# Small matmuls of a token mixer on halves and quarters of TensorE, two DMA queues at the start, and one norm's total in another PSUM bank

## The chip, the cores and the metric

One core of one Trainium2 chip runs the whole program once per launch. The metric is the time of one execution in microseconds, measured on the device; lower is better. The engines are TensorE (PE, with its weight loads shown apart as PEld), VectorE (DVE), ScalarE (ACT), GpSimd (POOL) and SyncE (SP), which issues most DMAs.

## The reference, cut to what matters

Two transformer-like layers run on 16 learned meta tokens and 256 real tokens of width 1024, all in float32.

```python
# layer 1: the mixer, then the expert layer
proj = rmsnorm(h, norm1_g) @ w_in     # 1024 -> q,k,v (8 heads x 64), q,k (4 x 64), v, gate (4 x 128), 16 low-rank gate inputs
log_1m  = where(mask, log_sigmoid(-z), 0)              # stick-breaking attention: z = q k^T / 8, strictly causal
between = cumsum(log_1m, reverse) - log_1m
sb_o    = where(mask, exp(log_sigmoid(z) + between), 0) @ v
lg      = log_sigmoid(glr @ w_gate_up + b) / 16        # glr: the 16 low-rank gate inputs
gla_o   = gated_linear_attention(q / 8, k, v, lg)      # decays are exp of differences of cumsum(lg)
h += concat(rmsnorm(sb_o), rmsnorm(gla_o) * silu(gate)) @ w_out
h += peer_ffn(rmsnorm(h, norm2_g))                     # scores of 2 x 8 x 128 sub-keys, top 16 of 256 pairs, 16384 experts
# layer 2, on the meta tokens of its own and rmsnorm(h, norm_f_g)
q, k, v, q_idx, k_idx, w_idx, conv..., gates... = split(rmsnorm(h, norm_mix_g) @ w_in_2)
sel   = top_k(sum_heads(relu(q_idx k_idx^T) * w_idx), 68)   # which keys a query may see
mixed = sigmoid(ga) * (attention(q, k, v, sel) @ w_attn_out) + sigmoid(gb) * (short_conv(...) @ w_conv_out)
h += mixed @ w_out;  h += (silu(f @ w_gate) * (f @ w_up)) @ w_down;  return rmsnorm(h)
```

## The kernel before

Activations lie transposed: 128 features on the partitions, tokens in the columns. A large product is made from halves: ScalarE casts a weight unit of 128x1024 from `raw_t` to fp32r (`hi_t`, L209), VectorE makes the rest (`lo_t`, L211), and TensorE adds three products per 128 rows, hi·hi, hi·lo and lo·hi (`mm3`, L226 to L228). A projection of 128 output columns is so 24 matmuls (`proj`, L230). Small products (attention scores, weighted values, transposes) run on plain float32, where each matmul of the program stands as two instructions in the trace.

The program is one stream without loops on the chip. A scheduler orders the instructions of each engine by its own estimates of durations, from the order in which the code is written and from the buffers that the pools give; engines then run their rows strictly in that order. Only the expert stage's VectorE part and the end of the expert stage are pinned by hand.

The start (L352 to L372) loads the gains `vec`, then the tokens `hx` in four pieces, with the first two weight units among them, all on SP's queue; `Feed.gains` (L1330) makes the halves `u` of the tokens and `Feed.then` (L1336) the squares, whose total (L1346) gives the norm's factor `rn`. A projection doesn't wait for `rn`: its result is multiplied by it afterwards (`put`, L404).

`mix_heads` (L374) first makes the gate `sil` (four projections, units 20 to 23), then the 16 low-rank inputs `glr` from a unit padded to 128 columns (L492), and from these the decays (L498). Then its loop over c (L603) interleaves value projections, one stick-breaking head at a time (`sb_head`, L431: three score matmuls L438 to L440 with 64 rows of contraction, the weights, three value matmuls L461 to L463) and the levels of the gated linear attention. `gla_head` (L591) sums four products per head, the first with only 16 rows of contraction (L595). Heads 6 and 7 come in the tail, beside the output projection.

The expert stage starts with eight projections and the sub-key scores (`scores`, L672), whose PSUM tiles come from the pool `pep` of two banks (L833). In layer 2, `norm_mix_scale` (L1088) takes two banks `st_t` at once, one for the total of the second norm and one (`ps2`) for that of the first norm, which `first()` fills only at the eighth k projection (L1164). The selection (`select`, L962) takes its banks `lg_t` from the pool that is opened after it (L1151).

Of the kernel before, what the change touches and what calls it, by code (L numbers as in the profile page):

```python
# [8 lines left out]
F32 = mybir.dt.float32  # L9
# [4 lines left out]
OP = mybir.AluOpType  # L14
# [85 lines left out]
def arrange(i):  # L100
# [12 lines left out]
    o["w1"] = _units(np.concatenate([w, np.zeros((D, 112), np.float32)], 1))  # L113
    o["wgu"] = np.ascontiguousarray(a["w_gate_up"][0])
# [22 lines left out]
class Net:  # L137
# [236 lines left out]
    def mix_heads(self, pool, tmp, feed, hx, h1, follow):  # L374
# [14 lines left out]
        glr = hp.tile([NM, L], F32, name="glr")  # L389
# [32 lines left out]
        def turned():  # L422
            for vf, c, blocks in waiting:
# [3 lines left out]
                for i, (dst, a, n) in enumerate(blocks):  # L427
                    nc.scalar.copy(dst[:, c * 128:(c + 1) * 128], tp[:n, i * 128:(i + 1) * 128])
            waiting.clear()

        def sb_head(h):  # L431

            c, pb = h // 2, 64 * (h % 2)
            P = slice(pb, pb + 64)
            k, q = sbk[P, c, :], sbq[P, c, :]
            z = bank("z")
            zz = z[:, 0:416]
            nc.tensor.matmul(z[:, 0:256], k[:, 0:128], q, start=True, stop=True)  # L438
            nc.tensor.matmul(z[:, 256:400], k[:, 128:256], q[:, 112:256], start=False, stop=True, skip_group_check=True)
            nc.tensor.matmul(z[:, 400:416], k[:, 144:272], q[:, 240:256], start=False, stop=True, skip_group_check=True)  # L440
# [17 lines left out]
            nc.scalar.activation(a, a, AF.Exp)  # L458
            o = bank("o")
            cs = slice(c * 128, (c + 1) * 128)  # L460
            nc.tensor.matmul(o[:, 0:256], sv[0][:, cs], a[:, 0:256], start=True, stop=True)  # L461
            nc.tensor.matmul(o[:, 112:256], sv[1][:, cs], a[:, 256:400], start=False, stop=True, skip_group_check=True)
            nc.tensor.matmul(o[:, 240:256], sv[2][:, cs], a[:, 400:416], start=False, stop=True, skip_group_check=True)  # L463
            nc.vector.tensor_copy(osb[P, c, :], o[P, 0:256])

# [23 lines left out]
        wgu = hp.tile([16, 256], F32, name="wgu")  # L489
        nc.sync.dma_start(wgu, t["wgu"])  # L490

        put(glr, self.proj(t["w1"][24], x, L)[:16, :], 0)  # L492
# [37 lines left out]
        am = pool.tile([NM, 2, 2, T], F32, name="am")  # L530
# [19 lines left out]
        def gla_pairs():  # L550
# [36 lines left out]
            for j, ps in enumerate(out):  # L587
                nc.vector.tensor_copy(am[:, j], ps[:NM])
# [14 lines left out]
        for c in range(4):  # L603
            value(8, c, [(sv[0], 0, 128), (sv[1], 128, 128), (sv[2], 144, 128)])
            next(gla, None)
            if c:
                sb_head(2 * c - 2)
# [3 lines left out]
            if c:  # L611
                sb_head(2 * c - 1)
# [12 lines left out]
        with tc.tile_pool(name="mxa", bufs=1, space=PSUM) as pacc:  # L625
# [13 lines left out]
            sb_head(6)  # L639
            mix_out(0)  # L640
            gla_head(2)
            sb_head(7)
# [179 lines left out]
    def experts(self, h, follow):  # L822
# [4 lines left out]
        with ExitStack() as es:  # L827
# [5 lines left out]
            psp = xs.enter_context(tc.tile_pool(name="pep", bufs=2, space=PSUM))  # L833
# [254 lines left out]
    def norm_mix_scale(self, psp):  # L1088
# [3 lines left out]
        ps, ps2 = (psp.tile([128, 512], F32, name="st_t", tag="st") for _ in range(2))  # L1092
# [8 lines left out]
        def first():  # L1101
            sq = self.sq
# [284 lines left out]
```

## Time and profile before

| what | us |
|---|---|
| median of 3 runs (lowest, highest) | 1440.45 (1439.87, 1441.21) |
| the profiled execution's own time | 1440.71 |
| its span in the trace | 1438.9 |
| TensorE busy, of the span | 1419.5 |
| VectorE busy | 1126.8 |
| ScalarE busy | 769.4 |

The span begins with the first instruction of any engine. Matmuls overlap one another, so a busy time near the span doesn't say that TensorE is at its peak; what a matmul costs in a stream is read from the distance between the starts of neighbouring rows. The stages are the mixer to about 165 us, the experts to about 940 us, and layer 2 after that.

### The profile page before, as it was taken

The numbers are of one execution on the slowest core, as the hardware profiler recorded it, in microseconds if no ns is written. First come the engines' busy times: TensorE is split into PE (matmuls) and PEld (weight loads), VectorE is DVE, ScalarE is ACT, GpSimd is POOL, SyncE is SP. The second block draws the span as 40 slices with busy tenths as digits, with TensorE's granted clock in tenths as the row PEclk, the third lists the DMA queues.
The fourth block names the chain that finished last, engine by engine and source line by source line (L and its number), as shares of the span: only waits on it lengthen the run. The fifth ranks groups of instructions, "written<-read, shape, count | busy, mean of one in ns | idle before, by whom it ended". The sixth has DMA issues, their size and how long they took to land. (4 is left out here: it accounts for less than half of the span.)

```text
span 1438.9 us, 25131 instructions
## 1 busy us (share of the span) xinstructions
PE 1419.5 (99%) x9846; PEld 1302.0 (90%) x9846; DVE 1126.8 (78%) x1920; ACT 769.4 (53%) x1241; POOL 0.2 (0%) x4
## 2 busy tenths in 40 slices
PE   7999999999999999999999999999999999999998
PEld 7998999999999999888888888898999888989997
DVE  6975889989979998687777777798767768776665
ACT  6656654445456665545445444554445556755554
POOL 0000000000000000000000000000000000000000
PEclk9999999999999999999999999999999999999999
DMA  7322556666655555787777777744533555565552
GB/s 280 118 103 95 166 173 227 229 227 225 218 190 187 193 184 190 244 257 251 244 242 241 241 241 240 234 144 147 171 137 132 178 189 193 174 220 190 181 187 72
DMA packets 86631, 279.05 MB, mean 194 GB/s; under 512 B 9760, under 2 KB 10480, under 8 KB 86384
## 3 DMA queue, kind: packets, MB, share of 16 engines
q1 hardware_dynamic: 77296, 260.67, 54.7%
q10 hardware_dynamic: 9216, 16.78, 3.1%
q8 instruction: 77, 1.26, 0.4%
q14 instruction: 42, 0.34, 0.1%
HBM read 259.52 MB, written 17.83 MB: 193 GB/s over the span
## 5 line engine op out<-in xcount | busy, mean ns | idle before, releaser
L211 DVE TENSOR_TENSOR lo_t<-raw_t,hi_t 128x1024 fp32r<-128x1024 f32 x456 | 554.4, 1221 | 137.0 <-ACT hi_t L209 134.6
L209 ACT CAST hi_t<-raw_t 128x1024 fp32r<-128x1024 f32 x456 | 476.2, 1049 | 302.9 <-PE mm_t L227 219.1
L226 PE MATMUL mm_t<-yh,hi_t 128*128 128x256 f32 x1024 | 292.9, 286 | 0.0
L228 PE MATMUL mm_t<-yh,lo_t 128*128 128x256 f32 x1024 | 290.3, 284 | 0.2 <-DVE lo_t L211 0.2
L227 PE MATMUL mm_t<-yl,hi_t 128*128 128x256 f32 x1024 | 289.8, 283 | 0.0
L312 PE MATMUL acc<-hi_t,vl_t 128*128 128x512 f32 x512 | 199.6, 390 | 0.0
L311 PE MATMUL acc<-lo_t,vh_t 128*128 128x512 f32 x512 | 199.5, 390 | 0.0
L310 PE MATMUL acc<-hi_t,vh_t 128*128 128x512 f32 x512 | 199.5, 390 | 0.0
L228 PEld LDWEIGHTS mm_t<-yh,lo_t 128*128 128x128 f32 x1024 | 196.3, 192 | 1.1 <-DVE lo_t L211 0.9
L227 PEld LDWEIGHTS mm_t<-yl,hi_t 128*128 128x128 f32 x1024 | 196.5, 192 | 0.1
L226 PEld LDWEIGHTS mm_t<-yh,hi_t 128*128 128x128 f32 x1024 | 196.4, 192 | 0.2
L246 PE MATMUL mm_t<-oo,hi_t 128*128 128x512 f32 x384 | 135.5, 395 | 0.0
L218 ACT CAST vh_t<-va_t 128x512 fp32r<-128x512 f32 x64 | 39.7, 621 | 152.2 <-DVE va_t L932 149.6
L311 PEld LDWEIGHTS acc<-lo_t,vh_t 128*128 128x128 f32 x512 | 96.1, 188 | 20.5 <-DVE lo_t L211 0.5
L312 PEld LDWEIGHTS acc<-hi_t,vl_t 128*128 128x128 f32 x512 | 96.1, 188 | 20.4 <-DVE vl_t L219 0.6
L310 PEld LDWEIGHTS acc<-hi_t,vh_t 128*128 128x128 f32 x512 | 96.1, 188 | 19.9
L226 PE MATMUL mm_t<-u,hi_t 128*128 128x272 f32 (+1 forms) x352 | 103.3, 295 | 7.9 <-ACT hi_t L209 7.5
L228 PE MATMUL mm_t<-u,lo_t 128*128 128x272 f32 (+1 forms) x352 | 102.4, 292 | 0.5 <-DVE lo_t L211 0.5
L227 PE MATMUL mm_t<-u,hi_t 128*128 128x272 f32 (+1 forms) x352 | 101.8, 290 | 0.0
L246 PE MATMUL mm_t<-oo,lo_t 128*128 128x256 f32 x384 | 100.4, 282 | 0.3 <-DVE lo_t L211 0.3
L246 PE MATMUL mm_t<-ax,hi_t 128*128 128x512 f32 x256 | 92.9, 399 | 0.0
L246 PEld LDWEIGHTS mm_t<-oo,hi_t 128*128 128x128 f32 x384 | 70.6, 188 | 12.7
(399 smaller groups left out, 2524.3 us busy)
## 6 DMA issues: line engine op xcount, KB each, us to landing
raw_t<-in_eu SPq DMA_DIRECT2D x128, 512.0 KB, 3.9
raw_t<-in_ev SPq DMA_DIRECT2D x128, 512.0 KB, 4.3
raw_t<-in_w2c SPq DMA_DIRECT2D x40, 512.0 KB, 3.4
act<-ge_t ACTq DMA_DIRECT2D x64, 256.0 KB, 3.3
va_t<-act SPq DMA_DIRECT2D x64, 256.0 KB, 3.2
raw_t<-in_w SPq DMA_DIRECT2D x25, 512.0 KB, 3.9
raw_t<-in_w2qkv SPq DMA_DIRECT2D x24, 512.0 KB, 4.1
raw_t<-in_wg SPq DMA_DIRECT2D x22, 512.0 KB, 3.5
```

The costliest lines, as they stand in the source:

```text
L209: nc.scalar.copy(hi, raw)
L211: nc.vector.tensor_tensor(lo, raw, hi[:].bitcast(F32), op=OP.subtract)
L218: self.nc.scalar.copy(hi, x)
L226: nc.tensor.matmul(ps, hi[:, ks], xhi[:, k, s], start=k == 0, stop=False)
L227: nc.tensor.matmul(ps, hi[:, ks], xlo[:, k, s], start=False, stop=False)
L228: nc.tensor.matmul(ps, lo[:, ks], xhi[:, k, s], start=False, stop=k == KC - 1)
L246: nc.tensor.matmul(out, w, y, start=k == 0 and out is pair, stop=k == KC - 1 and out is pair, skip_group_check=True)
L310: mm(acc[q], ah, hi, start=first, stop=False, skip_group_check=True)
L311: mm(acc[q], ah, lo, start=False, stop=False, skip_group_check=True)
L312: mm(acc[q], al, hi, start=False, stop=last, skip_group_check=True)
```

## The change

Seven edits are made together. (1) `vec` and the first weight unit (20) go on ScalarE's DMA queue, the unit in two pieces of 128x512 which are split apart from each other; the table load follows the DMA issues. (2) TensorE multiplies a tile of zeros 18 times before its first data. (3) `glr` comes from eight float32 matmuls with 32 output columns, each on one quarter of the array's columns, with unsplit weights `wlr`; the four partial sums lie on four groups of partitions and are added by the next matmul, whose weights are repeated. (4) `glr`, `gvm`, `am` and `wgu` are padded with zeros to 128 rows. (5) The scores of two stick-breaking heads are issued in turns, on the upper and the lower 64 rows, into two banks; their values are issued in turns on the left and right 64 columns of the array, into one bank that one copy empties. (6) The expert pool `pep` has four banks. (7) The first norm's total is put in a bank of the matmul pool, taken when it is needed.

```diff
@@ arrange
-    o["w1"] = _units(np.concatenate([w, np.zeros((D, 112), np.float32)], 1))
-    o["wgu"] = np.ascontiguousarray(a["w_gate_up"][0])
+    o["w1"] = _units(w[:, :3072])
+    o["wlr"] = _cols(np.concatenate([w[:, 3072:], np.zeros((D, 16), np.float32)], 1))
+    o["wgu"] = np.tile(np.concatenate([a["w_gate_up"][0], np.zeros((16, 256), np.float32)], 0), (4, 1))
@@ consts
-        nc.sync.dma_start(vec, self.t["vec"])
+        nc.scalar.dma_start(vec, self.t["vec"])
@@ mixer
-        self.act_table(LNEXP)
...
+            whi, wlo = self.turns[0]
+            self.turns = self.turns[1:] + self.turns[:1]
+            first = [self.raw.tile([128, 1024], F32, name="raw_t", tag="raw")]
+            first += [whi.tile([128, 1024], F32R, name="hi_t", tag="hi"), wlo.tile([128, 1024], F32R, name="lo_t", tag="lo")]
+            self.early.append(tuple(first[1:]))
+            w = t["w1"][20].rearrange("p k j -> p (k j)")
+            parts = [[x[:, 512 * i:512 * i + 512] for x in first] for i in range(2)]
             for k in range(0, KC, 2):
                 nc.sync.dma_start(hx[:, k:k + 2, :], t["hx"][:, k:k + 2, :])
-                if not k:
-                    self.early.append(self.unit(t["w1"][20]))
-                feed.gains((k, k + 1))
-                if not k:
-                    self.early.append(self.unit(t["w1"][21]))
+                if k < 4:
+                    nc.scalar.dma_start(parts[k // 2][0], w[:, 256 * k:256 * k + 512])
+            self.act_table(LNEXP)
+            with tc.tile_pool(name="idle", bufs=1) as ip:
+                idle = ip.tile([128, 256], F32R, name="idle")
+                nc.vector.memset(idle[:].bitcast(F32), 0.0)
+                ps = self.bank()
+                for _ in range(18):
+                    nc.tensor.matmul(ps[:, :256], idle[:, :128], idle, start=True, stop=True)
+            feed.gains((0, 1))
+            for i, (raw, hi, lo) in enumerate(parts):
+                self.split(hi, lo, raw)
+                feed.gains((2 * i + 2, 2 * i + 3))
+            feed.gains((6, 7))
+            self.early.append(self.unit(t["w1"][21]))
@@ mix_heads
-        gvm = pool.tile([NM, 512], F32, name="gvm")
+        gvm = pool.tile([128, 512], F32, name="gvm")
+        nc.gpsimd.memset(gvm, 0.0)
...
-        def sb_head(h):
...
+        def sb_scores(c):
+            zs = [bank("z") for _ in range(2)]
+            for a, n, b, m, o in ((0, 128, 0, 256, 0), (128, 256, 112, 256, 256), (144, 272, 240, 256, 400)):
+                for i, z in enumerate(zs):
+                    P = slice(64 * i, 64 * i + 64)
+                    nc.tensor.matmul(z[:, o:o + m - b], sbk[P, c, a:n], sbq[P, c, b:m], start=o == 0, stop=True, skip_group_check=True)
+            return zs
...
+        def sb_values(c, heads):
+            o = bank("o")
+            for v, b, a, n in ((sv[0], 0, 0, 256), (sv[1], 112, 256, 144), (sv[2], 240, 400, 16)):
+                for i, w in enumerate(heads):
+                    nc.tensor.matmul(o[64 * i:64 * i + 64, b:b + n], v[:, c * 128 + 64 * i:c * 128 + 64 * i + 64], w[:, a:a + n],
+                                     start=b == 0, stop=True, skip_group_check=True)
+            nc.vector.tensor_copy(osb[:, c, :], o[:, 0:256])
...
-        put(glr, self.proj(t["w1"][24], x, L)[:16, :], 0)
+        nc.vector.tensor_tensor(wlr, wlr, n1, op=OP.mult)
+        ps = self.bank()
+        for k in range(KC):
+            i = 32 * (k % 4)
+            nc.tensor.matmul(ps[i:i + 32, :L], wlr[:, k, :], hx[:, k, :], start=k < 4, stop=k > 3, skip_group_check=True)
+        put(glr, ps[:, :L], 0)
...
-        am = pool.tile([NM, 2, 2, T], F32, name="am")
+        am = pool.tile([128, 2, 2, T], F32, name="am")
+        nc.gpsimd.memset(am, 0.0)
@@ experts
-            psp = xs.enter_context(tc.tile_pool(name="pep", bufs=2, space=PSUM))
+            psp = xs.enter_context(tc.tile_pool(name="pep", bufs=4, space=PSUM))
@@ norm_mix_scale
-        ps, ps2 = (psp.tile([128, 512], F32, name="st_t", tag="st") for _ in range(2))
+        ps = psp.tile([128, 512], F32, name="st_t", tag="st")
...
-            sq = self.sq
+            sq, ps2 = self.sq, self.bank()
```

The scheduler moves rows with it. On TensorE, in the mixer's loop, heads 0 and 1 of the stick-breaking attention stood like this before (`z_t` are score banks, `o_t` value banks, `sbq` and `sbk` queries and keys, `a` the weights, `sv0` to `sv2` the values):

```order
L438 MATMUL z_t_671<-sbq_146,sbk_147 128x256
L439 MATMUL z_t_671<-sbq_146,sbk_147 128x144
L440 MATMUL z_t_671<-sbq_146,sbk_147 128x16
L226 MATMUL mm_t_700<-u_92,hi_t_703 128x256
...
L438 MATMUL z_t_757<-sbq_146,sbk_147 128x256
L439 MATMUL z_t_757<-sbq_146,sbk_147 128x144
L440 MATMUL z_t_757<-sbq_146,sbk_147 128x16
...
L461 MATMUL o_t_695<-a_692,sv0_152 128x256
L462 MATMUL o_t_695<-a_692,sv1_153 128x144
L463 MATMUL o_t_695<-a_692,sv2_154 128x16
```

and in the same place of the changed kernel:

```order
L456 MATMUL z_t_682<-sbq_174,sbk_175 128x256
L456 MATMUL z_t_683<-sbq_174,sbk_175 128x256
L456 MATMUL z_t_682<-sbq_174,sbk_175 128x144
L456 MATMUL z_t_683<-sbq_174,sbk_175 128x144
L456 MATMUL z_t_682<-sbq_174,sbk_175 128x16
L456 MATMUL z_t_683<-sbq_174,sbk_175 128x16
...
L487 MATMUL o_t_787<-a_707,sv0_180 64x256
...
L487 MATMUL o_t_787<-a_784,sv0_180 64x256
L487 MATMUL o_t_787<-a_707,sv1_181 64x144
L487 MATMUL o_t_787<-a_784,sv1_181 64x144
L487 MATMUL o_t_787<-a_707,sv2_182 64x16
L487 MATMUL o_t_787<-a_784,sv2_182 64x16
```

The score rows of the two heads now alternate in one group, while of the value rows head 0's first stands alone, 20 rows ahead of the other five.

On TensorE at the end of the expert projections, the sub-key scores (`sc_t`) stood in four groups with matmuls of the first expert block (`yh`, `yl`) between them:

```order
L684 MATMUL sc_t<-sk,pq 128x128 x8
L226 MATMUL mm_t<-yh,hi_t 128x256
L227 MATMUL mm_t<-yl,hi_t 128x256
L228 MATMUL mm_t<-yh,lo_t 128x256
L226 MATMUL mm_t<-yh,hi_t 128x256
L684 MATMUL sc_t<-sk,pq 128x128 x8
```

and in the changed kernel:

```order
L229 MATMUL mm_t<-u,lo_t 128x256
L729 MATMUL sc_t<-sk,pq 128x128 x32
L227 MATMUL mm_t<-yh,hi_t 128x256
L228 MATMUL mm_t<-yl,hi_t 128x256
L229 MATMUL mm_t<-yh,lo_t 128x256
```

All 32 now stand in one group.

On VectorE in layer 2, among the last k projections (`k` is the product with the norm's factor, `lo_t` the rest of the next weight unit), the rows were:

```order
L1159 TENSOR_TENSOR k<-mm_t,r_10904 128x272
L211 TENSOR_TENSOR lo_t<-raw_t,hi_t 128x1024
L1159 TENSOR_TENSOR k<-mm_t,r_10904 128x272
L211 TENSOR_TENSOR lo_t<-raw_t,hi_t 128x1024
L1159 TENSOR_TENSOR k<-mm_t,r_10904 128x272
```

and in the changed kernel (`sc` are selection scores, `top` and `left` its rounds of eight maxima):

```order
L1204 TENSOR_TENSOR k<-mm_t,r_10906 128x272
L1036 MAX top_11280<-left_11279 128x8
L1055 MEMSET lgs_12014 128x2x112
L1037 MATCH_REPLACE left_11279<-top_11280,left_11279 128x148
L212 TENSOR_TENSOR lo_t<-raw_t,hi_t 128x1024
L1036 MAX top_11280<-left_11279 128x8
L1055 MEMSET lgs_12015 128x2x112
L1037 MATCH_REPLACE left_11279<-top_11280,left_11279 128x148
L1204 TENSOR_TENSOR k<-mm_t,r_10906 128x272
```

The selection's first half, which stood behind the eighth k projection, now runs among the k projections.

## Rows read from the trace of the kernel before

**Rows 1.** The page's part 1 (busy, share, instructions) and the clock row of part 2.

```profile
PE 1419.5 (99%) x9846; PEld 1302.0 (90%) x9846; DVE 1126.8 (78%) x1920; ACT 769.4 (53%) x1241; POOL 0.2 (0%) x4
...
PEclk9999999999999999999999999999999999999999
```

**Rows 2.** Waits of TensorE: row and releaser, total us, times, longest.

```profile
PE mm_t L226 <- ACT hi_t L209: 7.5, 1, 7.5
```

**Rows 3.** Timeline of the start: start us, us, engine, line, operation, tiles.

```profile
4.01 0.93 ACT L1333 ACTIVATE u<-hx,vec 128x272 fp32r<-128x272 f32 x2 [2.00 <-DMA hx<-in_hx]
...
6.37 1.04 ACT L209 CAST hi_t<-raw_t 128x1024 fp32r<-128x1024 f32 x1 [0.88 <-DMA raw_t<-in_w]
...
7.47 0.58 PE L226 MATMUL mm_t<-u,hi_t 128*128 128x256 f32 x1 [7.47 <-ACT hi_t L209]
...
12.60 1.03 ACT L209 CAST hi_t<-raw_t 128x1024 fp32r<-128x1024 f32 x1
...
13.58 0.41 PE L228 MATMUL mm_t<-u,lo_t 128*128 128x256 f32 x1
...
14.10 1.03 ACT L209 CAST hi_t<-raw_t 128x1024 fp32r<-128x1024 f32 x1
...
14.39 0.28 PE L228 MATMUL mm_t<-u,lo_t 128*128 128x256 f32 x1
...
17.68 1.08 PE L1346 MATMUL g_t<-sums,con 128*128 128x272 f32 x4
```

**Rows 4.** DMA traffic from 0 to 40 us, in slices of 1 us.

```profile
GB/s 0 35 148 330 389 334 356 369 386 413 424 485 417 423 381 420 422 401 332 385 90 0 0 147 360 16 217 336 274 303 336 213 336 274 254 78 0 16 8 250
```

**Rows 5.** Timeline of TensorE: the decays' matmul and a float32 group.

```profile
29.40 1.31 PE L498 MATMUL mm_t<-glr,wgu 16*128 16x272 f32 x4
30.87 0.40 PE L226 MATMUL mm_t<-u,hi_t 128*128 128x272 f32 x1 [0.17 <-ACT lg L499]
...
42.92 1.16 PE L556 MATMUL g_t<-gq,gk 64*128 64x128 f32 x16
```

**Rows 6.** Timeline of TensorE: the scores of one stick-breaking head.

```profile
57.32 0.65 PE L438 MATMUL z_t<-sbq,sbk 64*128 64x256 f32 x2
...
58.27 0.39 PE L226 MATMUL mm_t<-u,hi_t 128*128 128x256 f32 x1
58.50 0.28 PE L227 MATMUL mm_t<-u,hi_t 128*128 128x256 f32 x1
```

**Rows 7.** Timeline of TensorE: the values of one stick-breaking head.

```profile
66.04 0.64 PE L461 MATMUL o_t<-a,sv 128*128 128x256 f32 x2
...
66.90 0.37 PE L226 MATMUL mm_t<-u,hi_t 128*128 128x272 f32 x1
```

**Rows 8.** Timeline of TensorE: one head of the gated linear attention.

```profile
122.58 0.69 PE L595 MATMUL o_t<-am,gvm 16*128 16x256 f32 x2
123.20 0.49 PE L596 MATMUL o_t<-at,gv 128*128 128x128 f32 x2
123.53 0.39 PE L597 MATMUL o_t<-at,gv 128*128 128x128 f32 x2
123.75 0.39 PE L598 MATMUL o_t<-a,gv 128*128 128x128 f32 x2
```

**Rows 9.** Timeline of TensorE: the sub-key scores' first group, and their end.

```profile
183.93 1.16 PE L684 MATMUL sc_t<-sk,pq 64*128 64x128 f32 x16
...
191.59 0.39 PE L226 MATMUL mm_t<-yh,hi_t 128*128 128x256 f32 x1
```

**Rows 10.** Timeline of ScalarE beside them: the copies of two score tiles.

```profile
185.12 1.07 ACT L687 COPY S<-sc_t 128x512 f32<-128x512 f32 x2
```

**Rows 11.** Busy us (and instructions) of each engine in two stretches of layer 2.

```profile
963.00:986.00 23.00, 23.00 (x179) 22.76 (x178) 19.39 (x38) 11.94 (x19) 0.00 (x0) 1.00 0.49 161
986.00:1025.00 39.00, 38.10 (x238) 31.96 (x237) 38.37 (x114) 18.73 (x41) 0.00 (x0) 1.00 0.41 136
```

**Rows 12.** VectorE on the tiles `top` alone, from 986 to 1025 us.

```profile
986.00:1025.00 39.00, 14.24 (x54) 1.00 0.41 136
```

More of the change, by code (lines that the diff above doesn't have):

```diff
@@ L388, in mix_heads @@
         sil = pool.tile([128, 4, T], F32, name="sil")
-        glr = hp.tile([NM, L], F32, name="glr")
+        glr = hp.tile([128, L], F32, name="glr")
         sv = [hp.tile([128, 512], F32, name=f"sv{b}") for b in range(3)]
         gv = [pool.tile([128, 512], F32, name=f"gv{b}") for b in range(2)]
-        gvm = pool.tile([NM, 512], F32, name="gvm")
+        gvm = pool.tile([128, 512], F32, name="gvm")
+        nc.gpsimd.memset(gvm, 0.0)
         osb = pool.tile([128, 4, T], F32, name="osb")
@@ L427, in turned, with sb_weights @@
                 for i, (dst, a, n) in enumerate(blocks):
-                    nc.scalar.copy(dst[:, c * 128:(c + 1) * 128], tp[:n, i * 128:(i + 1) * 128])
+                    nc.scalar.copy(dst[:n, c * 128:(c + 1) * 128], tp[:n, i * 128:(i + 1) * 128])
             waiting.clear()
-        def sb_head(h):
[L433 to L436, printed above, removed]
+        def sb_scores(c):
[5 more added lines that the diff above has]
+            return zs
+        def sb_weights(z):
             zz = z[:, 0:416]
-            nc.tensor.matmul(z[:, 0:256], k[:, 0:128], q, start=True, stop=True)
-            nc.tensor.matmul(z[:, 256:400], k[:, 128:256], q[:, 112:256], start=False, stop=True, skip_group_check=True)
-            nc.tensor.matmul(z[:, 400:416], k[:, 144:272], q[:, 240:256], start=False, stop=True, skip_group_check=True)
             zm = hp.tile([128, 416], F32, name="zm", tag="zm", bufs=3)
@@ L458, in sb_head, with sb_heads @@
             nc.scalar.activation(a, a, AF.Exp)
+            return a
+        def sb_values(c, heads):
             o = bank("o")
[L460 to L464, printed above, removed]
+            for v, b, a, n in ((sv[0], 0, 0, 256), (sv[1], 112, 256, 144), (sv[2], 240, 400, 16)):
[3 more added lines that the diff above has]
+            nc.vector.tensor_copy(osb[:, c, :], o[:, 0:256])
+        def sb_heads(c):
+            zs = sb_scores(c)
+            heads = [sb_weights(zs[0])]
+            yield
+            heads.append(sb_weights(zs[1]))
+            sb_values(c, heads)
+            yield
         def head_norm(o, c, w, d, g, hi, lo, gate=None):
@@ L488, in mix_heads @@
         nc.scalar.copy(tri, self.c("negtri"))
-        wgu = hp.tile([16, 256], F32, name="wgu")
+        wgu = hp.tile([128, 256], F32, name="wgu")
         nc.sync.dma_start(wgu, t["wgu"])
-        put(glr, self.proj(t["w1"][24], x, L)[:16, :], 0)
+        wlr = hp.tile([128, KC, 32], F32, name="wlr")
+        nc.sync.dma_start(wlr, t["wlr"])
+        n1 = self.vec[:, VEC["n1"]:VEC["n1"] + KC].unsqueeze(2).broadcast_to([128, KC, 32])
+        nc.vector.tensor_tensor(wlr, wlr, n1, op=OP.mult)
[4 more added lines that the diff above has]
+        put(glr, ps[:, :L], 0)
         put(gq[:, 0, :], self.proj(t["w1"][12], x, T, real), NM, 0.125)
@@ L587, in gla_pairs @@
             for j, ps in enumerate(out):
-                nc.vector.tensor_copy(am[:, j], ps[:NM])
+                nc.vector.tensor_copy(am[:NM, j], ps[:NM])
             yield
@@ L606, in mix_heads @@
             if c:
-                sb_head(2 * c - 2)
+                sb = sb_heads(c - 1)
+                next(sb)
             put(sbq[:, c, :], self.proj(t["w1"][c], x, T, real), NM, 0.125)
@@ L611, in mix_heads @@
             if c:
-                sb_head(2 * c - 1)
+                next(sb)
             put(sbk[:, c, :], self.proj(t["w1"][4 + c], x, L), 0)
@@ L638, in mix_heads @@
             head_norm(og, 0, "ones", 128.0, "glag", *gh, sil)
-            sb_head(6)
+            sb = sb_heads(3)
+            next(sb)
             mix_out(0)
             gla_head(2)
-            sb_head(7)
+            next(sb)
             mix_out(1)
```

## The prediction

> **What bounds the kernel now.** I read the page's busy times first [rows 1]: TensorE is busy 1419.5 us, 99% of the span. Its waits come second [rows 2]: the one that matters is 7.5 us at the start, and nothing later is over a few tenths. So the time is TensorE's row stream after a start, and an edit pays where it shortens that stream or begins it sooner, as long as VectorE and ScalarE keep up. Third is the timeline where the edits lie: the start [rows 3], the small matmuls of the mixer [rows 5 to 8], the sub-key scores [rows 9, 10] and layer 2 [rows 11, 12]. Busy times don't price small matmuls, since neighbours overlap, so I take distances between starts. Two of them serve throughout: 96 matmuls of projections stand between 30.87 and 42.92 [rows 5], 0.1255 us each, and the float32 pair of 256 columns on the full array is priced with its followers below.
>
> **Start.** Before, the first matmul waits until 7.47 for the cast of unit 20, whose data came at 6.37 [rows 3]. The matmuls then last 0.41 us until 13.58 and 0.28 from 14.39: TensorE is at the lower of its two clock levels (1.2 against 2.4 GHz) for nearly 7 us after its first work, though the granted clock of the page reads full from the first slice [rows 1]. The change gives the first piece of the unit to a second queue. By the traffic of rows 4, summed, 0.51 MB had moved by 4.0, 0.90 by 5.0 and 1.24 by 6.0; tokens of 0.28 MB, `vec` and a piece of 0.26 MB can so be in at about 5.3 with the delay that the first cast shows (0.84 MB were needed at 6.37). With a cast of half the length (estimate 0.6, from 1.04) the first data matmul starts near 6.1. The zeros (18 x 0.21 at the lower level) run from about 1.2 to 5, so with the same delay the clock is up near 8. But TensorE is then fed slower than it works. ScalarE still makes the same gains, casts and squares in its order, and as before the casts of units 22 and 23 can't end before about 13.6 and 15.1 [rows 3]. What is gained is the backlog: units 20 and 21 (48 matmuls) are done by about 13.7, and the norm's total, which now stands behind 54 matmuls and needs the last squares, comes at about 15.9 instead of 17.68. I take 1.8 us; from 0, if the weights of units 22 and 23 set the pace anyway, to 3.5, if earlier data let ScalarE start 1.7 sooner.
>
> The traffic reaches 389 GB/s while only one queue issues [rows 4], so the engines behind the queues are already shared. The Trainium skill (Trainium Kernel Development and Optimization, Key Constraints) says that DMAs of all queues run on the same 16 engines, and that a second queue only saves issue time. By that the term would be near 0.5 us and the time 1434.8; this trace has one input queue at the start and cannot decide it.
>
> **The 16 gate inputs.** 24 matmuls of 0.1255 go: 3.0 us, with a load, a cast and a subtraction that lie beside TensorE. Eight float32 matmuls come, 16 instructions of 272 columns. A full-array pair of 256 columns with followers of 144 and 16 takes 0.86 [rows 7]; by columns the pair is about 0.47, so one instruction of 272 is 0.25. One after the other that is 4.0, four abreast 1.0. Each matmul's second instruction must wait for its first on the same quarter, so I expect two abreast: 2.1, and 0.2 for changing the shape. Saved 0.7 (-1.2 to 1.8). **Decays:** four instructions of 16 rows take 1.47 [rows 5]; four of 0.25 on the full array 1.0. Saved 0.5 (0.2 to 0.6). **Linear attention:** the product with 16 rows takes 0.62, the next pair 0.33, where the same pair without a change of shape takes 0.22 [rows 8]. Full height makes this 0.47 and 0.22: 0.26 for each of four heads, 1.0 (0 to 1.2).
>
> **Scores.** A head costs 0.95 [rows 6], a pair 1.9. That the two halves of the rows work at once is seen in rows 5: 16 instructions of 128 columns in 1.16, when 0.235 x 128/256 x 16 = 1.9 would be one after the other. In turns a pair is 0.9 and an edge of 0.25, saved 0.75. The order keeps it whole for the first two pairs; in the third, another product stands between the two long rows (0.5 saved), in the tail the two heads stay apart (nothing). 2.0 in sum (-0.3 to 3.3).
>
> **Values.** A head costs 0.86 [rows 7], a pair 1.72. The order puts head 0's long row alone: 0.47 and a change of shape, then the other five, about 0.72 and a change. With 64 rows the same columns take 0.95 instead of 0.86, and the first matmul after them is followed at 0.23 (58.27 to 58.50) instead of 0.1255 [rows 6, 7]: about 0.2 for a visit. So 1.6 a pair, saved 0.1 each, 0.4 in sum (-1.0 to 2.4, the latter if the rows met as in the scores).
>
> The change of shape costs 0.2 here [rows 6]. The Trainium skill (TensorEngine Tiling (Array Packing), Key Properties) says why: a change of the tiling mode drains TensorE. It speaks against the values, which were on the full array and now visit another mode twice a pair, eight drains in all; with no work abreast to pay them the term would be -1.6, by the row's 0.2.
>
> **Sub-key scores.** Four groups of 16 instructions and 12 matmuls between take 7.66 us, from 183.93 to 191.59 [rows 9], because each group waits for the two copies that free its banks, 1.07 [rows 10]. With four banks the 32 stand together; the third and fourth groups still wait for copies, so about 4.5, then the 12 matmuls at 0.12: 5.9. Saved 1.7 (0 to 2.3).
>
> **First norm's bank.** Layer 2's selection can begin as soon as its queries are there, since no bank of the closed pool is held until the eighth k projection. VectorE has 3.6 us free between 963 and 986 and 0.6 between 986 and 1025, while TensorE loses 0.9 there [rows 11]. The rounds of maxima cost 14.24 for both halves [rows 12]; the first half (144 of 416 columns, with fixed costs, estimate 6) and its scoring (3 at most) move into the first stretch: 9 against 3.6, 5.4 too many, and the second stretch is relieved by as much. TensorE holds two prepared weight units, 48 matmuls of 0.1255, 6.0 us, against such a lag. I take 0 (-5 to 3).
>
> **Waits given back.** In the tail the chain of heads 6 and 7 through ScalarE and VectorE doesn't get shorter, TensorE's filler does; I take off 1.0 (0 to 2). VectorE loses four copies, a subtraction of 1.2 and gains little; GpSimd's two fills lie beside everything.
>
> Sum: 1.8 + 0.7 + 0.5 + 1.0 + 2.0 + 0.4 + 1.7 + 0 - 1.0 = 7.1 us. The profiled execution took 1440.71, so 1433.6; that execution lies 0.26 over the median, and I say 1433.5.
>
> **Rivals.** *The parts of the array don't work side by side* in this order (the change doesn't do what it says). Rows 5 speak against it for halves of the rows; for parts of the columns no row speaks. Then the gate inputs cost 1.2, scores lose 0.3 and values 1.0: 7.1 - 1.9 - 2.3 - 1.4 = 1.5, 1439.2. *The other engines set the pace:* the gains of the mixer become waits on the chain of weights between scores and values, and the start gains nothing. For it: ScalarE's order at the start is nearly unchanged. Against it: TensorE has no wait after the start. Left are decays, linear attention and sub-key scores, 3.2, and 0.3 of the rest: 1437.2. *Layer 2's selection comes too early:* VectorE's 5.4 us too many come where weights must be prepared, and the total's bank is one of the two that projections use in turn, so that a late reader behind the rounds of maxima stalls the next two, each for up to its 24 x 0.1255 = 3.0. If all of it falls on TensorE the cost is 11.4: 1440.7 - 7.1 + 11.4 = 1445.0, slower. It decides once VectorE lags by more than the 6.0 of prepared weights; for it speaks that VectorE is busy 38.37 of 39 already, against it that the second stretch gets the time back. *More is gained:* the start at 3.5, quarters four abreast, layer 2 at +3: 13 us, 1427.7.
>
> **How the numbers follow.** A difference under 0.2% (2.9 us, 1437.6 to 1443.3 around the median) can't be told from none. Forecast (gain of 4.5 to 10 us) 0.57; more 0.09; the parts apart 0.12; the pace of the others 0.12; the selection 0.10, of which 0.07 slower by over 0.2% and 0.03 within. The parts apart would come within, but the spread of the other terms puts 0.04 of their 0.12 over 2.9; of the pace of the others, at 3.3, it leaves 0.08 there. Faster 0.57 + 0.09 + 0.04 + 0.08 = 0.78, within 0.08 + 0.04 + 0.03 = 0.15, slower 0.07. The range leaves out most of the slower case and the far end of the gain: 1428.5 to 1439.5.
>
> **What would show it.** In the profile after: data matmuls of 0.28 us from the first on, first at about 6, the norm's total near 16; eight matmuls of `wlr` in about 2.3; score groups of two heads in about 1.15; values no shorter than 1.5 a pair; the sub-key scores in one group of about 4.5; and no wait over 1 us on `lo_t` between the k projections. I am wrong if the stretch before 165 gains under 4 us, or if layer 2 moves by more than 3 either way.

## The result, and the profile after

The changed kernel takes 1431.83 us (median of 4 runs, 1431.58 to 1432.62), the kernel before 1440.82 beside it: a ratio of 0.9943 (0.9931 to 0.9954). 1433.5 was forecast, with 1428.5 to 1439.5 as the range. The profiled execution took 1432.62, its span is 1430.8, so 8.1 us went from the span.

The busy row of the page answers to [rows 1]:

```profile
PE 1414.2 (99%) x9856; PEld 1295.5 (91%) x9856; DVE 1125.3 (79%) x1918; ACT 767.1 (54%) x1241; POOL 1.6 (0%) x6
```

The waits of TensorE (row, releaser, total us, times, longest) answer to [rows 2]; the one long wait has become several short ones. The first is that of the zeros for their own memset; `sp` is the step between a stick-breaking head's scores and its weights, `rel_t` the relu of the selection's scores:

```profile
PE mm_t L380 <- DVE idle L377: 1.2, 1, 1.2
PE mm_t L227 <- ACT hi_t L219: 1.1, 1, 1.1
PE mm_t L229 <- DVE lo_t L212: 0.9, 2, 0.7
...
PE z_t L476 <- ACT sp L219: 0.6, 1, 0.6
PE lg_t L1021 <- ACT rel_t L1024: 0.6, 1, 0.6
```

TensorE's timeline after, in the columns of [rows 3], at the places of [rows 3] and [rows 5 to 9] (`xN` counts instructions, two for each plain float32 matmul of the program):

```profile
1.22 3.73 PE L380 MATMUL mm_t<-idle 128*128 128x256 f32 x18 [1.22 <-DVE idle L377]
6.05 0.39 PE L227 MATMUL mm_t<-u,hi_t 128*128 128x256 f32 x1 [1.10 <-ACT hi_t L219]
...
7.00 0.28 PE L227 MATMUL mm_t<-u,hi_t 128*128 128x256 f32 x1
...
12.45 0.39 PE L229 MATMUL mm_t<-u,lo_t 128*128 128x256 f32 x1 [0.74 <-DVE lo_t L212]
...
15.85 1.08 PE L1391 MATMUL g_t<-sums,con 128*128 128x272 f32 x4
...
21.84 1.12 PE L533 MATMUL mm_t<-hx,wlr 128*32 128x272 f32 x16
22.89 0.39 PE L227 MATMUL mm_t<-u,hi_t 128*128 128x256 f32 x1
...
25.84 1.41 PE L540 MATMUL mm_t<-glr,wgu 128*128 128x272 f32 x4
27.41 0.40 PE L227 MATMUL mm_t<-u,hi_t 128*128 128x272 f32 x1 [0.16 <-ACT lg L541]
...
53.87 1.03 PE L456 MATMUL z_t<-sbq,sbk 64*128 64x256 f32 x12
54.83 0.39 PE L227 MATMUL mm_t<-u,hi_t 128*128 128x256 f32 x1
...
64.26 0.65 PE L487 MATMUL o_t<-a,sv 128*64 128x256 f32 x2
64.83 0.39 PE L229 MATMUL mm_t<-u,lo_t 128*128 128x272 f32 x1
...
67.77 0.96 PE L487 MATMUL o_t<-a,sv 128*64 128x256 f32 x10
68.67 0.40 PE L229 MATMUL mm_t<-u,lo_t 128*128 128x272 f32 x1
...
118.19 0.60 PE L638 MATMUL o_t<-am,gvm 128*128 128x256 f32 x2
118.63 0.38 PE L639 MATMUL o_t<-at,gv 128*128 128x128 f32 x2
118.85 0.39 PE L640 MATMUL o_t<-at,gv 128*128 128x128 f32 x2
...
159.42 1.03 PE L1391 MATMUL sc_t<-sums,con 128*128 128x256 f32 x4
...
178.32 4.45 PE L729 MATMUL sc_t<-sk,pq 64*128 64x128 f32 x64
182.70 0.39 PE L227 MATMUL mm_t<-yh,hi_t 128*128 128x256 f32 x1
...
943.70 0.62 PE L1391 MATMUL st_t<-sums,con 128*128 128x256 f32 x2
...
1422.45 1.06 PE L1332 MATMUL mm_t<-sql,con 128*128 128x256 f32 x4
```

Read as distances to the start of the next row: the 16 instructions of the gate inputs take 1.05 (21.84 to 22.89), a pair of heads 0.96 for its scores and 0.57 + 0.90 for its values, the product with `am` 0.44 and the next 0.22, the sub-key scores 4.38 in one group.

Four marks cut the span into stages that can be compared between kernels: the gate inputs' first row, the totals `sc_t` (mixer's end) and `st_t` (experts' end), and the last total. In the kernel before they stand here:

```profile
23.46 0.29 PE L226 MATMUL mm_t<-u,hi_t 128*128 128x272 f32 x1
...
165.03 1.04 PE L1346 MATMUL sc_t<-sums,con 128*128 128x256 f32 x4
...
951.63 0.62 PE L1346 MATMUL st_t<-sums,con 128*128 128x256 f32 x2
...
1430.82 1.06 PE L1287 MATMUL mm_t<-sql,con 128*128 128x256 f32 x4
```

The differences of such rows, in us, and the medians of the runs:

| kernel | start, to the gate inputs | mixer | experts | layer 2 | median |
|---|---|---|---|---|---|
| before | 23.46 | 141.57 | 786.60 | 479.19 | 1440.82 |
| after | 21.84 | 137.58 | 784.28 | 478.75 | 1431.83 |
| e1, one zero matmul | 21.75 | 137.55 | 784.32 | 478.29 | 1432.12 |
| e2, one queue | 22.46 | 137.64 | 784.22 | 478.29 | 1432.78 |
| e3, one quarter | 21.30 | 140.20 | 784.12 | 478.38 | 1434.19 |
| e4, values on the full array | 22.07 | 138.13 | 784.24 | 478.32 | 1432.62 |
| e5, unit 21 early | 24.03 | 137.51 | 784.17 | 479.98 | 1435.27 |
| e6, the same, one zero | 23.60 | 137.49 | 784.54 | 478.25 | 1434.84 |
| e7, bank back | 20.88 | 137.52 | 784.73 | 479.20 | 1432.82 |
| e8, values held | 21.24 | 134.88 | 784.81 | 479.84 | 1429.85 |
| e9, held, start by order alone | 22.47 | 135.33 | 784.48 | 478.28 | 1431.12 |
| e10, scores apart | 21.18 | 140.36 | 785.04 | 478.31 | 1433.55 |
| e11, 16 rows again | 20.84 | 138.66 | 784.79 | 478.43 | 1434.14 |
| e12, two banks `pep` | 21.66 | 137.54 | 786.11 | 479.98 | 1435.03 |

So the change won 1.62 in the start, 3.99 in the mixer, 2.32 in the experts and 0.44 in layer 2, 8.37 in all; behind the last total 0.3 was lost. The table also shows what can't be told from it. Kernels with one and the same start differ by 1.2 in the first column (20.84 to 22.07), those with the same four banks by 0.9 in the experts (784.12 to 785.04), and layer 2, the same rows in all but two of them, by 1.7. The mixer is steadier: seven kernels with the same rows there lie within 0.15 (137.49 to 137.64), e8 and e9 0.45 apart. The stages are those of one profiled execution each. The medians come from different sets of runs, beside which the kernel before took 1440.33 (e1 to e4), 1440.53 (e5 to e8) and 1440.92 (e9 to e12). A part of under 1 us is read from the stage that it changes, not from the time.

### The profile page after: what moved, and what is told of

Read it like the earlier page. It is cut to its first block, busy times and chain, and to the rows that moved or that the text cites. A ratio compares the mean times of both kernels' runs of the same rounds, so it can differ in the third digit from the quotient of the medians.

```text
span 1430.8 us, 25145 instructions
## 1 busy us (share of the span) xinstructions
PE 1414.2 (99%) x9856; PEld 1295.5 (91%) x9856; DVE 1125.3 (79%) x1918; ACT 767.1 (54%) x1241; POOL 1.6 (0%) x6
## 4 chain that ended last, share of the span: by engine, by line
PE 94%; DVE 3%; ACT 2%; DMA 1%; issue 1%; ACTq 0%; DVEq 0%
PE mm_t L247 18%; PE mm_t L227 13%; PE mm_t L229 12%; PE mm_t L228 12%; PE acc L313 8%; PE acc L312 8%; PE acc L311 8%; PE acc L282 2%; PE acc L283 2%; PE acc L281 2%; PE ga_t L849 1%; PE ga_t L850 1%; DVE lo_t L212 1%; PE tp_t L350 0%; DMA raw_t<-in_w 0%
## 5 line engine op out<-in xcount | busy, mean ns | idle before, releaser
L227 PE MATMUL mm_t<-u,hi_t 128*128 128x272 f32 (+1 forms) x344 | 100.6, 293 | 2.3 <-ACT hi_t L219 1.1
L229 PE MATMUL mm_t<-u,lo_t 128*128 128x272 f32 (+1 forms) x344 | 99.2, 289 | 1.0 <-DVE lo_t L212 0.7
L228 PE MATMUL mm_t<-u,hi_t 128*128 128x272 f32 (+1 forms) x344 | 98.6, 287 | 0.3 <-DVE u L1379 0.3
```

The source lines that it names most:

```text
L227: nc.tensor.matmul(ps, hi[:, ks], xhi[:, k, s], start=k == 0, stop=False)
L228: nc.tensor.matmul(ps, hi[:, ks], xlo[:, k, s], start=False, stop=False)
L229: nc.tensor.matmul(ps, lo[:, ks], xhi[:, k, s], start=False, stop=k == KC - 1)
```

## The experiments

All start from the changed kernel (e6 from e5, e9 from e8).

**e1, the zeros.**

```diff
-                for _ in range(18):
+                for _ in range(1):
```

> The changed kernel with one matmul on zeros in place of 18; all rows of the other engines stand as they were. Theory, the clock: in the kernel before TensorE's matmuls were slow until 14.2 us, 6.9 after its first work at 7.47. Without the zeros the data matmuls from 6.05 on would be slow (0.22 to 0.24 from start to start) until about 12.9, and the norm's total would come at about 16.7 instead of 15.85: the time rises by 0.5 to 1.0 us. Rival, the feed: ScalarE and VectorE, which prepare weights and tokens, end their last squares at 15.6 with or without zeros, so slow matmuls only fill waits: total within 0.2 of 15.85, time the same. Second rival, all 1.8 us of the start come from the zeros: total at 17.7, +1.8.

1432.12 us. TensorE's timeline of e1:

```profile
6.91 0.58 PE L227 MATMUL mm_t<-u,hi_t 128*128 128x256 f32 x1 [5.12 <-ACT hi_t L219]
...
8.24 0.42 PE L228 MATMUL mm_t<-u,hi_t 128*128 128x256 f32 x1
...
11.85 0.28 PE L227 MATMUL mm_t<-u,hi_t 128*128 128x256 f32 x1
...
15.76 1.08 PE L1391 MATMUL g_t<-sums,con 128*128 128x272 f32 x4
```

The matmuls last 0.41 until shortly before 11.85, and still the norm's total comes at 15.76: the slow ones only fill what were waits. The rival holds, the zeros are worth next to nothing here. In the ten other profiles with unit 21 behind the tokens, TensorE's last wait at the start is for that unit's rest (12.45 in the changed kernel), and the gate inputs stand 9.39 to 9.44 behind it. In e1 TensorE waits for nothing after 6.91. VectorE ended that rest at 12.09 there and at 12.40 in the changed kernel, so by the same distance the gate inputs could have stood at about 21.5 (an estimate) instead of 21.75: the zeros were worth 0.2 at the most. In e8 and e10, whose starts have the same rows as the changed kernel's, the 18 zeros didn't even bring the short matmuls (0.41 at 7.92 in e8, in its timeline below), and e8's total came at 15.26.

**e2, the second queue.**

```diff
-        nc.scalar.dma_start(vec, self.t["vec"])
+        nc.sync.dma_start(vec, self.t["vec"])
...
-                    nc.scalar.dma_start(parts[k // 2][0], w[:, 256 * k:256 * k + 512])
+                    nc.sync.dma_start(parts[k // 2][0], w[:, 256 * k:256 * k + 512])
```

> The changed kernel with the gains and the two halves of the first weight unit issued on SyncE's queue again, between the tokens' pieces; the two halves and the zeros stay. The scheduler then sets two of the squares earlier on ScalarE. Theory, shared DMA engines (as the Trainium skill, Trainium Kernel Development and Optimization, Key Constraints, has it): the same bytes come in the same time, only the issue of about 0.5 us is saved by the second queue: first data matmul between 6.0 and 6.6, time within 0.5 us of the changed kernel. Rival, the second queue brings the weights earlier by itself: first data matmul at 7 or later, time 1 us or more longer.

1432.78 us. The first data matmul starts at 5.85, no later than with two queues, as the Trainium skill's sentence on queues that share the engines (Trainium Kernel Development and Optimization, Key Constraints) would have it. The median lies 0.95 over the changed kernel's, more than the theory's 0.5, though the intervals of the two ratios overlap (0.9934 to 0.9962 and 0.9931 to 0.9954). The mark after the start stands at 22.46, 0.4 behind the latest of the others with the start of the change. ScalarE's timeline of the changed kernel at unit 21's cast:

```profile
10.11 1.03 ACT L210 CAST hi_t<-raw_t 128x1024 fp32r<-128x1024 f32 x1
```

and of e2:

```profile
10.14 0.64 ACT L1384 ACTIVATE sq_t<-hx 128x544 f32<-128x544 f32 x1
10.69 1.04 ACT L210 CAST hi_t<-raw_t 128x1024 fp32r<-128x1024 f32 x1
```

ScalarE has finished the tokens' halves at the same time in both (10.11 and 10.14), although in e2 it has made two squares by then. The scheduler puts a third square ahead of unit 21's cast, which so begins 0.58 later, and TensorE gets the rest of the unit at 13.03 instead of 12.45. In these two profiles the delay is the order of the squares, and the single queue costs nothing that can be seen.

**e5 and e6, the order of the transfers.**

```diff
                 nc.sync.dma_start(hx[:, k:k + 2, :], t["hx"][:, k:k + 2, :])
+                if not k:
+                    raw21 = self.load(t["w1"][21])
...
-            for i, (raw, hi, lo) in enumerate(parts):
+            for raw, hi, lo in parts:
                 self.split(hi, lo, raw)
-                feed.gains((2 * i + 2, 2 * i + 3))
-            feed.gains((6, 7))
-            self.early.append(self.unit(t["w1"][21]))
+            self.early.append(self.halve(raw21))
+            feed.gains((2, 3, 4, 5, 6, 7))
```

> The changed kernel with the second weight unit (21) loaded right behind the first piece of tokens and cast ahead of the remaining tokens, as in the kernel before; the first unit's halves on the second queue and the zeros stay. Theory, the transfer order carries the start's gain: tokens and their halves come late again, the norm's total stands at 17.0 us or later (15.85 in the changed kernel) and the time rises by 1.0 to 1.8. Rival, several edits each suffice: at the high clock level the 48 matmuls of units 20 and 21 need 5.8 us and are done by about 15.1 in either order, total within 0.5 of 15.85, time within 0.4.

> The kernel of the run with unit 21 early, with one matmul on zeros in place of 18. Theory, several edits each suffice, and this one takes away the second of them: TensorE's data matmuls are slow (0.21 apart) from about 7 until 12 or 13, now with work waiting for them, so the total comes at 16.8 to 17.6 and the time is 0.7 to 1.6 us over that of its partner with 18 zeros. Rival, the feed sets the pace whatever the order: total and time within 0.3 us of the partner.

1435.27 and 1434.84 us. TensorE's timeline of e5:

```profile
7.70 0.28 PE L228 MATMUL mm_t<-u,hi_t 128*128 128x256 f32 x1
...
9.00 0.58 PE L227 MATMUL mm_t<-u,hi_t 128*128 128x256 f32 x1 [0.90 <-ACT hi_t L210]
...
15.54 0.28 PE L227 MATMUL mm_t<-u,hi_t 128*128 128x256 f32 x1
...
18.27 1.08 PE L1392 MATMUL g_t<-sums,con 128*128 128x272 f32 x4
```

and the engines of e5 from 9 to 15 (busy us and instructions of PE, PEld, DVE, ACT, POOL, then granted clock, DMA share, GB/s):

```profile
9.00:15.00 6.00, 5.75 (x25) 5.45 (x26) 5.90 (x10) 6.00 (x12) 0.00 (x0) 0.50 1.03 421
```

With unit 21 ahead of the tokens the whole gain of the start is gone (24.03 and 23.60 against 23.46 before), halves, second queue and zeros notwithstanding. e6 and e1, which differ in this order alone, stand 1.85 apart (23.60 and 21.75). In e5 TensorE worked at the high level, waited for the next cast until 9.00, and then ran at a granted clock of 0.50, 1.2 GHz, until after 15. So my rival for e5 was not put to its test: it took the high level for granted. Nor was my theory for e6, since its partner was slow as well (and 0.4 later). Once TensorE is slow in this order it sets the pace itself: it waits for nothing after 10.26 in e5, 10.54 in e6 and 8.73 before, and its matmuls last 0.41 until about 15, 14 and [rows 3] 13.58. The place of unit 21 thus costs time by waits and, behind them, by the clock; what this order would take at the high level no run shows.

**e9, the order alone** (with e8's values).

```diff
...
-                if k < 4:
-                    nc.scalar.dma_start(parts[k // 2][0], w[:, 256 * k:256 * k + 512])
+                if not k:
+                    nc.sync.dma_start(first[0], w)
...
-                feed.gains((2 * i + 2, 2 * i + 3))
-            feed.gains((6, 7))
+            self.split(first[1], first[2], first[0])
+            feed.gains((2, 3, 4, 5, 6, 7))
```

> The kernel with the held values (1429.85 us), with the start of the kernel before in all but one thing: gains and first unit on SyncE's queue again, the first unit in one piece, one matmul on zeros in place of 18; only the second unit's load and cast stay behind the tokens and their halves. Theory, the order of the transfers carries the start's gain: the gate inputs' group stands within 1.2 us of its place with the full start (21.24) and the time within 0.8 of 1429.85. Rival, the halves of the first unit carry it: the first data matmul comes at 7 us or later, the group at 22.9 or later, 1.5 us or more slower.

1431.12 us; first data matmul at 6.71, mark at 22.47. It is 1.0 ahead of the kernel before and 1.2 behind e8; the time is 1.27 over e8. Neither number holds wholly: the place of unit 21's load and cast alone brings 1.0, the other edits together another 0.4 to 1.6 (against 20.84 to 22.07). As in e2, the scheduler sets squares ahead of unit 21's cast (two, from 9.34 to 10.43), and TensorE waits 0.37 for the unit's rest at 13.04, so the squares account for 0.37 at most. What of the remainder is the halves, the zeros or the second queue is open.

**e3, quarters of the columns.**

```diff
...
-            i = 32 * (k % 4)
-            nc.tensor.matmul(ps[i:i + 32, :L], wlr[:, k, :], hx[:, k, :], start=k < 4, stop=k > 3, skip_group_check=True)
+            nc.tensor.matmul(ps[:32, :L], wlr[:, k, :], hx[:, k, :], start=k == 0, stop=k == KC - 1)
...
```

> The changed kernel with all eight gate-input matmuls on the first quarter of the columns, summed there, in place of two on each quarter; the other three quarters of the result are zeros. The order of TensorE's rows is the same. Theory, four quarters work abreast: the group that took 1.05 us takes 16 x 0.25 = 4.0 on one quarter, and the time rises by 2 to 3 us. Rival, a matmul of 32 columns is short by itself: the group takes 1.0 to 1.5 and the time stays within 0.3 us.

1434.19 us; timeline of e3:

```profile
21.30 3.85 PE L533 MATMUL mm_t<-hx,wlr 128*32 128x272 f32 x16
...
25.08 0.38 PE L227 MATMUL mm_t<-u,hi_t 128*128 128x256 f32 x1
```

16 instructions in 3.78 on one quarter, 0.236 each, against 1.05 on four: the quarters work side by side, nearly fourfold. The mixer is 2.6 longer, as the theory says.

**e4 and e8, the values.** In e4 each head is again on the full array; in e8 one exponential gives the weights of both heads, so that no value row is ready alone:

```diff
@@ sb_weights
             nc.vector.tensor_tensor(a, zz, self.c("sbmask"), op=OP.min)
-            nc.scalar.activation(a, a, AF.Exp)
@@ sb_heads
+            a = hp.tile([128, 2, 416], F32, name="a", tag="a", bufs=1)
+            sb_weights(zs[0], a[:, 0])
             yield
+            sb_weights(zs[1], a[:, 1])
+            nc.scalar.activation(a, a, AF.Exp)
+            sb_values(c, [a[:, 0], a[:, 1]])
```

> The changed kernel with the values of the stick-breaking heads on the full array again, each head by itself in its own bank and with its own copy. Theory, halves of the columns work abreast and pay for the two changes of shape: a pair of heads takes 1.72 us again instead of 1.47, four pairs: +1.0 us. Rival, the time won is given back in waits for the weights between scores and values: the time stays within 0.3 us. Second rival, the changes of shape cost more than the work abreast saves: 0.5 us or more faster.

> The changed kernel with the weights of a pair of stick-breaking heads in one tile and one exponential for both, so that the six value matmuls of a pair stand together in turns. Theory, the left and the right half of the columns then work side by side throughout: 12 instructions in about 1.15 us instead of 0.57 and 0.90 apart, with one visit of the other shape instead of two: 0.3 for each of four pairs, the time falls by 0.5 to 1.2 us. Rival, the head that is ready waits for the other and the chain through ScalarE and VectorE gives it back: within 0.3 us or slower.

e4: 1432.62 us, mixer 0.55 longer; the value rows themselves cost 1.22 more (7.11 against 5.89 from start to next start, all pairs), about half of it is not found again in the stage. By the time alone (+0.8, with overlapping intervals) it is undecided. e8: 1429.85 us, ratio 0.9926 (0.9913 to 0.994), by its median the fastest kernel of this study, though this interval overlaps the changed kernel's. Timeline of e8:

```profile
7.92 0.41 PE L227 MATMUL mm_t<-u,hi_t 128*128 128x256 f32 x1
...
66.86 0.97 PE L484 MATMUL o_t<-a,sv 128*64 128x256 f32 x12
67.76 0.39 PE L229 MATMUL mm_t<-u,lo_t 128*128 128x272 f32 x1
```

The 12 instructions of a pair take 0.90, where one head on the full array took 0.86 [rows 7]. The right half is all but free, and the mixer is 2.7 shorter (2.2 in e9, which has the same values), more than twice what I expected; 2.3 of it are the value rows (3.61 against 5.89).

**e10, scores one head after the other.**

```diff
-            for a, n, b, m, o in ((0, 128, 0, 256, 0), (128, 256, 112, 256, 256), (144, 272, 240, 256, 400)):
-                for i, z in enumerate(zs):
+            for i, z in enumerate(zs):
+                for a, n, b, m, o in ((0, 128, 0, 256, 0), (128, 256, 112, 256, 256), (144, 272, 240, 256, 400)):
```

> The changed kernel with the scores of a pair of heads written one head after the other instead of in turns, still on the upper and the lower rows and in two banks. Theory, only neighbours on different rows work side by side: the 12 instructions of the first two pairs take 1.7 to 1.9 us instead of 0.96, and the time rises by 1.5 to 2.3. Rival, the second head's rows start beside the first head's whatever the order: below 1.2 us a pair, time within 0.4.

1433.55 us; timeline of e10:

```profile
53.20 1.56 PE L456 MATMUL z_t<-sbq,sbk 64*128 64x256 f32 x12
54.69 0.39 PE L227 MATMUL mm_t<-u,hi_t 128*128 128x256 f32 x1
```

1.49 a pair, between theory (1.7) and rival (1.2): without turns the halves overlap in part. The mixer is 2.8 longer, of which the score rows are 1.4 (7.40 against 6.02) and the value rows 0.5 (6.37 against 5.89); the scheduler also moved other products of the loop, and the rest was not taken apart.

**e11, 16 rows of contraction.**

```diff
-        am = pool.tile([128, 2, 2, T], F32, name="am")
-        nc.gpsimd.memset(am, 0.0)
+        am = pool.tile([NM, 2, 2, T], F32, name="am")
```

(`gvm` likewise, and the copy into `am` takes the whole tile.)

> The changed kernel with the first product of each head of the gated linear attention on 16 rows again; the order of all rows stays. Theory, a product of 16 rows costs two changes of shape that the padded one spares: 0.62 and 0.33 instead of 0.44 and 0.22 for this product and the next, 0.3 for each of four heads, the time rises by 0.9 to 1.2 us. Rival, other waits of the tail take it up: within 0.3.

1434.14 us, with runs from 1432.11 to 1436.48. Timeline of e11:

```profile
117.23 0.69 PE L636 MATMUL o_t<-am,gvm 16*128 16x256 f32 x2
117.85 0.49 PE L637 MATMUL o_t<-at,gv 128*128 128x128 f32 x2
118.18 0.39 PE L638 MATMUL o_t<-at,gv 128*128 128x128 f32 x2
```

0.62 and 0.33 as foretold; the mixer is 1.08 longer. The three longest of the five executions (1434.14 to 1436.48) show a mean granted clock of 0.996 or 0.997, the two shortest (1432.11 and 1432.82) 0.998 and 0.999. So here the spread goes with the clock; where in those executions it fell, no profile shows.

**e12, the expert pool.**

```diff
-            psp = xs.enter_context(tc.tile_pool(name="pep", bufs=4, space=PSUM))
+            psp = xs.enter_context(tc.tile_pool(name="pep", bufs=2, space=PSUM))
```

> The changed kernel with two banks for the sub-key scores again. Theory, each group then waits for the copies that free its banks: four groups with 12 matmuls of the first expert block between them in about 7.7 us, where 4.4 and 1.4 make 5.8: the time rises by 1.5 to 2.1 us. Rival, the expert stage behind takes it up: within 0.4.

1435.03 us. The expert stage is 1.83 longer, as the theory says (1.1 to 2.0 against the other kernels with four banks). The rest of the time's 3.2 is mostly layer 2, 1.23 longer in this profile (below); the start is 0.2 shorter.

**e7, the first norm's bank.**

```diff
-        ps = psp.tile([128, 512], F32, name="st_t", tag="st")
+        ps, ps2 = (psp.tile([128, 512], F32, name="st_t", tag="st") for _ in range(2))
```

> The changed kernel with the first norm's total back in a bank of the pool of the norms, so that layer 2's selection begins again behind the eighth k projection. Theory, the bank moves rows but no time: layer 2 from its norm's total to the end takes 478.7 us in the changed kernel and 479.2 before; within 0.5 of that, time within 0.6 us of the changed kernel. Rival, the early selection overloads VectorE and costs TensorE waits that other edits hide: 1 us or more faster. Second rival, it relieves the later stretch and carries more of the gain than the traces show: 1 us or more slower.

1432.82 us. Layer 2 takes 479.20, as before (479.19). With the early selection it takes 478.25 to 478.75 in nine profiles and 479.84 to 479.98 in three (e5, e8, e12). What parts them is one place. e8 there, in the columns of e5's engines above, from the wait on:

```profile
959.00:961.00 2.00, 1.38 (x12) 1.01 (x12) 2.00 (x7) 1.96 (x5) 0.00 (x0) 1.00 0.00 0
...
963.00:965.00 2.00, 2.00 (x10) 2.00 (x10) 2.00 (x4) 0.29 (x1) 0.00 (x0) 0.50 0.86 272
```

and the same place in e9:

```profile
961.00:963.00 2.00, 1.38 (x7) 0.79 (x6) 2.00 (x5) 1.28 (x3) 0.00 (x0) 1.00 0.00 0
963.00:965.00 2.00, 2.00 (x12) 1.49 (x12) 2.00 (x5) 0.29 (x1) 0.00 (x0) 1.00 0.35 106
```

The early scoring makes TensorE wait for its own relu (`lg_t` on `rel_t`, 0.6) and work at 1.38 of 2 us. Behind this thin stretch the granted clock goes to 0.50, 1.2 GHz, in e8 (in e5 and e12 likewise), and stays at full in e9; in e7 the stretch is without a wait. The early selection so gains 0.4 to 0.9 where the clock holds and loses 0.7 where it falls: the theory "moves rows but no time" is right only on the mean of the twelve (478.76). That the thin stretch brings the fall is argued from its place, not shown: nine profiles have the stretch without the fall, and only two (before and e7) are without the stretch. Held values with the bank back were not run.

## Why the prediction was right

The working was right in the sum (7.1 forecast, 8.1 in the span) and in the mechanism of most terms; several sizes were off, and that the sum came within 1.0 is in part luck: the gate inputs (1.2 over), the values (0.6), the first norm's bank and the scores (0.4 each) made up for the decays (0.6 under) and the waits given back (1.1).

- **Start** (1.8): 1.83 at the norm's total, 1.62 at the gate inputs. The size held and so did its reason, that the other engines feed TensorE more slowly than it works (e1). But I gave the credit to data that come sooner by a second queue and to the level of the clock. e5, e6 and e9 show the place of unit 21 behind the tokens instead, which the working had not priced; the clock counts through it, since TensorE, which waits more in the old order, also worked slowly for longer there (until about 14 in e6, 11.7 in e1). Units 20 and 21 were done at 15.14 and not at 13.7, since TensorE had waited until 12.45 for unit 21's rest; that the total still came where I had put it, at 15.85, is partly luck. The first data matmul at 6.05 (6.1 forecast) is luck too: by the delay of the first cast, some 1.5 behind its bytes, the working should have had the data at 5.7 and not at 5.3. The rule on shared queues, by which I would have said 1434.8, agreed with e2's first matmul and with its halves of the tokens; it was no argument against the gain, since e2 shows nothing that the second queue carried.
- **Gate inputs** (0.7): 1.94 (5.94 from 23.46 to 29.40 before, 4.00 after). I took two quarters abreast, since each matmul's second instruction follows its first on the same quarter; it is four (e3). This is the term that was mis-sized most.
- **Decays** (0.5): nothing; 1.57 against 1.47. I took four instructions of 16 rows to be dear for their shape; on the full height they are no cheaper, and the 0.16 for `lg` stayed.
- **Linear attention** (1.0): 1.1 (e11).
- **Scores** (2.0): 2.35 (8.37 before, 6.02 after, from start to next start). A pair takes 0.96 instead of the 1.15 forecast.
- **Values** (0.4): 0.97 (6.86 to 5.89), the split row at 0.57 and not 0.67. A pair takes 1.47, a little under the 1.5 that I had set as the least. The Trainium skill's drain at a change of mode (TensorEngine Tiling (Array Packing), Key Properties) was my reason for -1.6 with no work abreast; work abreast paid for whatever the change of shape costs. I had read that cost from the first matmul behind a small group, followed at 0.23 instead of 0.1255, but behind a full-array group it was followed at 0.21 too (66.90 to 67.11 before). What differs more is the row ahead of the group, 0.21 instead of 0.13 (67.56 to 67.77 after, 65.91 to 66.04 before). The same section has tiles work independently, and e8 agrees: 0.90 for two heads.
- **Sub-key scores** (1.7): 1.83 (e12), one group of 4.38 where I said 4.5.
- **First norm's bank** (0): 0.44 in this profile, -0.8 to 0.9 over all of them, where the clock makes the difference. No wait over 1 us on `lo_t` came.
- **Waits given back** (1.0): 2.1. From the decays' end to the mixer's end the three terms above (2.35, 0.97 and 0.93 for the linear attention there) make 4.25, and the stage became 2.15 shorter (134.16 to 132.01). 1.0 of the rest is waits of TensorE (1.01 to 2.03), above all 0.6 for `sp`, which I put down to the shorter filler ahead of it; 0.7 is dearer products with `sp` (6.23 to 6.97), 0.4 lies scattered. What makes those products dearer was not tried.

The rivals fell where the runs reach them: the parts work side by side (e3, e8), TensorE remains the bound after the start (busy 1414.2 of 1430.8), and the selection's early rows cost no stall of weights, only a wait of 0.6 for their own relu and, in three profiles, what follows it.

## What to carry to other kernels

Matmuls that use half or a quarter of the columns pay most when they stand together in turns; here one exponential for both heads released them all, and the second half was nearly free (e8). At the start of a kernel look at what the first matmuls wait for in the order in which it is loaded and cast, and at what the scheduler puts ahead of that cast, before adding queues or warming the clock. Price parts of under 1 us by the distance between two marks around their stage.

## What the runs showed of the hardware

16 float32 instructions of 272 columns on 32 output columns take 3.78 us on one quarter of the array and 1.05 on four. Twelve instructions of two heads on halves of the columns take 0.90, on halves of the rows 0.96 in turns and 1.49 not in turns. TensorE's granted clock fell to 0.50 after a start at the high level with waits of 0.2 to 1.2 us (e5), and again in the midst of layer 2, behind two microseconds in which it was busy 1.38 with one wait of 0.6 (e8), and not behind the same stretch in e9. At the start of e8 the matmuls lasted 0.41 us while the clock's column read full, and as long as in e5 at a granted clock of 0.50, so the durations are the better witness there.
